# Four residual and four A12 buffers instead of two in the first down projection of a two-layer trunk

## Chip, cores and metric

The kernel runs on one core of one Trainium2 chip. The metric is the device time of one execution in microseconds (us); the median of three runs is given.

## What is computed

Two layers, each a mixer and a SwiGLU block, on 1024 tokens of width 1024 in float32. The reference, cut to what this change touches:

```python
def rmsnorm(x, g):
    y = x * lax.rsqrt(jnp.mean(x * x, axis=-1, keepdims=True) + RMS_EPS)
    return y * g
def swiglu(h, w_gate, w_up, w_down):
    return (jax.nn.silu(h @ w_gate) * (h @ w_up)) @ w_down
for layer in range(2):
    h = rmsnorm(x, norm_mix_pre[layer])
    m = attention_mixer(h, ...) if layer == 0 else recurrent_mixer(h, ...)
    x = x + rmsnorm(m, norm_mix_post[layer])
    h = rmsnorm(x, norm_ffn_pre[layer])
    x = x + rmsnorm(swiglu(h, ...), norm_ffn_post[layer])
```

The stage in question is the `@ w_down` of layer 0 with the norm and residual behind it, the pre-norm of layer 1's recurrent mixer, and that mixer's first projection (`h @ w_in`).

## The kernel before

Matrix products are done in float32 by splitting each operand into a high and a low half and adding three products (lines 748 to 750: high by high, high by low, low by high). The halves are made by a cast on ScalarE (ACT) and a subtraction on VectorE (DVE). A scheduler orders the instructions of each engine's queue from the program; buffers of a tag rotate, and an instruction that takes a buffer waits for the last reader of the tile that had it.

The down projection (`down`, lines 736 to 885) is one level of Strassen: seven products of 512 tokens by 512 columns with 11 steps of depth each. The first five (`p1`, `p6`, `p7`, `p5`, `p4`) leave the second half of the token rows (r = 1) finished, in four tiles `m2[0..3]` of 128 tokens. Each is then put through `norm(1, a, ...)`: `post_norm_of` (lines 234 to 263) loads the residual rows `x` (tag "nx", two buffers, line 241; line 196 issues the load), takes squares (ACT, line 178), gets 1/rms in two small instructions on GpSimd (POOL, lines 182 and 183), multiplies by the gain (DVE, line 250), adds the residual (DVE, line 256), stores `x` (line 258, SP's queue), and goes on to the pre-norm of the next mixer: squares of `x` (line 178), 1/rms, scaling (ACT, line 212), eight transposes on TensorE (PE, line 222, into two PSUM banks that rotate), a cast (ACT, line 57) and a subtraction (DVE, line 58) into `hT`.

While these norms run, PE does product `p3` (blocks S4, line 851, and w_down, line 855) and then the last product, token tile by token tile: for a = 0 to 3 the rows of A12 (from DRAM, line 875, tag "act", two buffers, three loads of 4, 4 and 3 blocks for each a) are split (ACT line 877, DVE line 878, into four buffers of tag "wb") and multiplied by the eleven split blocks `b21` (w_down, line 868), 33 matmuls for each a. DVE adds the result to `m1[a]` (line 883), and `norm(0, a, ...)` follows. Then the recurrent mixer starts: its weights are loaded (line 137, tag "raw", three buffers, shared with the loads of lines 851 and 868), scaled on DVE (line 151) or POOL (line 148), split (ACT line 155, DVE line 156), and the first projection (lines 166 to 168) multiplies them by `hT`: 72 matmuls on the first 512 tokens (a = 0 and 1), then 72 on the others (a = 2 and 3).

All loads and stores named here stand in SP's one queue, in the scheduler's order.

Of the kernel before, what the change touches and what calls it, by code (L numbers as in the profile page):

```python
# [8 lines left out]
F32 = mybir.dt.float32  # L9
# [6 lines left out]
P = 128  # L16
S = 1024
D = 1024
# [9 lines left out]
def rows(t, x):  # L28

    if not isinstance(t, tuple):  # L30
        return [(slice(0, P), x[t * P:(t + 1) * P, :])]
    r, a = t
    o = [2 * a * P + k * P + 64 * r for k in range(2)]
    return [(slice(64 * k, 64 * k + 64), x[o[k]:o[k] + 64, :]) for k in range(2)]


class HiddenT:


    def __init__(self, trunk, pool):  # L40
        self.nc = trunk.nc
        self.half = [tuple(pool.tile([P, KT, HALF], F32R, tag="hT", bufs=4, name=trunk.uid("hT"))
                           for _ in range(2)) for _ in range(2)]
# [56 lines left out]
class Trunk:  # L100
# [4 lines left out]
    def __init__(self, ctx, tc, io):  # L105
        self.ctx, self.tc, self.nc, self.io = ctx, tc, tc.nc, io
        nc = self.nc
        self.const = ctx.enter_context(tc.tile_pool(name="const", bufs=1))
        self.main = ctx.enter_context(tc.tile_pool(name="main", bufs=1))
        self.dram = ctx.enter_context(  # L110
            tc.tile_pool(name="dram", bufs=1, space=bass.MemoryType.DRAM))
        c = self.const
        self.ident = c.tile([P, P], F32, name="ident")
        make_identity(nc, self.ident)
        self.neghalf = c.tile([P, 1], F32, name="neghalf")
        nc.vector.memset(self.neghalf, -0.5)
        self.zero = c.tile([P, 1], F32, name="zero")
        nc.vector.memset(self.zero, 0.0)
        self.gcol = c.tile([P, 3, KT], F32, name="gcol")
        self.n = 0  # L120
        self.mark = None
        self.turned = {}
# [112 lines left out]
    def post_norm_of(self, ms, mg, x_src, x_dst, t, gpost, sink, pool, x=None):  # L235

        nc = self.nc
        if x is None:  # L240
            x = pool.tile([P, D], F32, tag="nx", bufs=2, name=self.uid("x"))
        for d, s in rows(t, x_src):
            self.load(x[d, :], s)
        junk = pool.tile([P, D // len(ms)], BF16, tag="junk", bufs=1, name=self.uid("junk"))

        squares_first = mg is ms[0][1] or len(ms) == 1
        if squares_first:
            rs = self.rstd(pool, [m for _, m in ms], junk)
        for c, m in ms:
            scaled = nc.vector.tensor_tensor(mg[:, c], m, gpost[:, c], op=ALU.mult).ins  # L250
        if not squares_first:
            rs = self.rstd(pool, [m for _, m in ms], junk)
        self.last_m = [self.squared, scaled]

        def rest(later=False):
            nc.vector.scalar_tensor_tensor(x, mg, rs, x, op0=ALU.mult, op1=ALU.add)
            for k, (d, s) in enumerate(rows(t, x_dst)):
                (nc.scalar if k and sink is None else nc.sync).dma_start(s, x[d, :])
            if sink is not None:
                return self.pre_norm(pool, x, mg, None, sink, t, self.psum_t, later)  # L260

        return rest
# [465 lines left out]
    def down(self, l, gO, x_src, x_dst, make_sink):  # L728
# [9 lines left out]
        def block(j, row, c0=0, n=D):  # L738
            return w[(2 * j + row) * P:(2 * j + row + 1) * P, c0:c0 + n]

        def split(pool, tag, bufs, src):
            t = pool.tile([P, 2, 512], F32R, tag=tag, bufs=bufs, name=self.uid("o"))
            nc.scalar.copy(t[:, 0], src)  # L743
            tt(t[:, 1], src, t[:, 0].bitcast(F32), op=ALU.subtract)  # L744
            return t

        def matmuls(ps, a, b, first, last):
            nc.tensor.matmul(ps, a[0], b[:, 0], start=first, stop=False)  # L748
            nc.tensor.matmul(ps, a[0], b[:, 1], start=False, stop=False)  # L749
            nc.tensor.matmul(ps, a[1], b[:, 0], start=False, stop=last)  # L750

        def product(operands, first=0):
            ps = [self.psum() for _ in range(4)]
            js = [*range(first, NP), *range(first)]
            for j in js:
                a, b = operands(j)
                for t in range(4):
                    tok = slice(t * P, (t + 1) * P)
                    matmuls(ps[t], (a[:, 0, tok], a[:, 1, tok]), b, j == js[0], j == js[-1])
            return ps  # L760

        main = self.main

        keep = make_sink is nullcontext
        with self.pool(f"d{l}") as ap, ExitStack() as right:
            m1, m2 = ([ap.tile([P, D], F32, tag="m", bufs=8, name=self.uid("m")) for _ in range(4)]
                      for _ in range(2))
# [68 lines left out]
            with make_sink() as sink:  # L836
                def norm(r, a, m):
                    ms, mg = [(slice(0, D), m)], m
                    if r == 0 and sink is None:
                        ms = [(c, m[:, c]) for c in (hi, lo)]  # L840
                        mg = ap.tile([P, D], F32, tag="mg", bufs=1, name=self.uid("mg"))

                    x = main.tile([P, D], F32, tag="raw", bufs=3, name=self.uid("x")) if keep and r == 0 else None
                    self.post_norm(ms, mg, x_src, x_dst, (r, a), gpost, sink, ap, x)

                for a in range(4):
                    norm(1, a, m2[a])

                def p3(j):
                    r = main.tile([P, 2, 512], F32, tag="raw", bufs=3, name=self.uid("raw"))  # L850
                    nc.sync.dma_start(r[:, 0], gO["S4"][j])
                    b22 = ts[j][:, 1]
                    if not keep:
                        b22 = r[:, 1]
                        nc.sync.dma_start(b22, block(j, 1, 512, 512))
                    return split(main, "w", 8, r[:, 0]), split(ap, "wb", 4, b22)

                for m, ps in zip(m1, product(p3)):
                    tt(m[:, hi], ps, m[:, hi], op=ALU.add)
                b21 = []  # L860
                for j in range(NP):
                    if keep:
                        src = ts[j][:, 0]
                    else:
                        if j % 2 == 0:
                            r = main.tile([P, 2, 512], F32, tag="raw", bufs=3, name=self.uid("raw"))
                        src = r[:, j % 2]
                        nc.sync.dma_start(src, block(j, 1, 0, 512))
                    b21.append(split(*((main, "w", 8) if j < 6 else (ap, "wc", 5)), src))
                for a in range(4):  # L870
                    ops = []
                    for j in range(0, NP, 4):
                        n = min(4, NP - j)
                        r = ap.tile([P, 4, P], F32, tag="act", bufs=2, name=self.uid("act"))[:, :n]
                        self.load(r, gO["A12"][:, j:j + n, a * P:(a + 1) * P])
                        t = ap.tile([P, 2, 4, P], F32R, tag="wb", bufs=4, name=self.uid("o"))
                        nc.scalar.copy(t[:, 0, :n], r)  # L877
                        tt(t[:, 1, :n], r, t[:, 0, :n].bitcast(F32), op=ALU.subtract)  # L878
                        ops += [(t[:, 0, i], t[:, 1, i]) for i in range(n)]
                    ps = self.psum()  # L880
                    for j in range(NP):
                        matmuls(ps, ops[j], b21[j], j == 0, j == NP - 1)
                    tt(m1[a][:, lo], ps, m1[a][:, lo], op=ALU.add)
                    norm(0, a, m1[a])
        self.mark = None


    def recurrent(self, ap, hT, yT):
# [275 lines left out]
```

## Time and profile before

| | us |
|---|---|
| median of 3 runs (lowest, highest) | 2204.94 (2204.70, 2206.01) |
| the profiled execution | 2205.06 |
| its span, first to last instruction | 2203.3 |
| TensorE busy in the span | 2170.1 |

Times inside the trace are us from the span's start. A matmul's record is longer than the step from one matmul to the next, since matmuls are pipelined; what PE takes is read from one start to the next. An ACT or DVE record likewise ends a little after the next one starts.

### The profile page before, as it was taken

To read this page: it belongs to the slowest core of one execution; us is meant where nothing else is said; L and a number is where in the kernel's file an instruction comes from. 1 tells how busy PE (TensorE), PEld (TensorE's weight loads), DVE (VectorE), ACT (ScalarE), POOL (GpSimd) and SP (SyncE) were. 2 spreads that over 40 slices of the span, in tenths; PEclk is the share of its full clock that TensorE was granted. 3 is DMA by queue.
4 is the path that set the end of the run, shared out by engine and by line. 5 is a ranking of instruction groups with operands and counts; after the bars stand their busy time and mean duration, and the time that the engine had idled before them with its cause. 6 is when DMAs were issued, how large, how long until landed. Compare 5 with 4: busy or idle time off the path is not lost.

```text
span 2203.3 us, 30597 instructions
## 1 busy us (share of the span) xinstructions
PE 2170.1 (98%) x11198; PEld 1811.7 (82%) x11198; DVE 1536.5 (70%) x2496; ACT 1143.0 (52%) x2108; POOL 228.2 (10%) x458
## 2 busy tenths in 40 slices
PE   8999999999999999999999999999999999999998
PEld 8898989878788888888887777887788888888886
DVE  6786765566868777676767677437777677768775
ACT  4545555466765444443446576527755444434543
POOL 3111112121100000000001332102100000000011
PEclk9999999999999999999999999999999999999999
DMA  5101011226323333336468421356233333328565
GB/s 177 54 30 35 25 54 38 65 85 219 137 91 101 117 95 119 96 129 229 144 181 251 127 62 40 95 195 222 81 111 106 95 120 96 120 95 287 170 179 158
DMA packets 184392, 266.03 MB, mean 121 GB/s; under 512 B 13617, under 2 KB 114993, under 8 KB 184242
## 3 DMA queue, kind: packets, MB, share of 16 engines
q1 hardware_dynamic: 183602, 261.98, 37.8%
q10 hardware_dynamic: 640, 2.10, 0.3%
q8 instruction: 88, 1.44, 0.3%
q14 instruction: 62, 0.51, 0.1%
HBM read 198.49 MB, written 65.54 MB: 120 GB/s over the span
## 4 chain that ended last, share of the span: by engine, by line
PE 85%; DVE 6%; ACT 3%; DMA 3%; issue 2%; POOL 1%; SPq 0%; POOLq 0%; ACTq 0%; DVEq 0%
PE ps L663 13%; PE ps L664 13%; PE ps L665 13%; PE ps L514 7%; PE ps L750 5%; PE ps L748 5%; PE ps L749 5%; PE psq L166 3%; PE psq L167 3%; PE psq L168 3%; PE pso L344 2%; PE tr L413 2%; PE ps L167 2%; PE ps L166 2%; PE ps L168 2%
## 5 line engine op out<-in xcount | busy, mean ns | idle before, releaser
L663 PE MATMUL ps<-hS,q 128*128 128x512 f32 (+1 forms) x1288 | 490.9, 382 | 0.3 <-ACT hS L96 0.3
L664 PE MATMUL ps<-hS,q 128*128 128x512 f32 (+1 forms) x1288 | 490.0, 381 | 0.9 <-DVE hS L89 0.9
L665 PE MATMUL ps<-hS,q 128*128 128x512 f32 (+1 forms) x1288 | 489.4, 380 | 0.0
L634 DVE TENSOR_TENSOR q<-raw,q 128x512 fp32r<-128x512 f32 x308 | 205.1, 688 | 191.8 <-ACT q L633 191.4
L664 PEld LDWEIGHTS ps<-hS,q 128*128 128x128 f32 x1288 | 243.3, 189 | 47.3 <-DVE hS L89 1.3
L663 PEld LDWEIGHTS ps<-hS,q 128*128 128x128 f32 x1288 | 243.0, 189 | 47.6 <-ACT hS L96 0.8
L665 PEld LDWEIGHTS ps<-hS,q 128*128 128x128 f32 x1288 | 243.2, 189 | 45.7
L633 ACT CAST q<-raw 128x512 fp32r<-128x512 f32 x308 | 177.0, 615 | 144.9 <-DVE raw L642 135.9
L749 PE MATMUL ps<-o,o 128*128 128x512 f32 x616 | 240.5, 391 | 0.2 <-DVE o L744 0.2
L750 PE MATMUL ps<-o,o 128*128 128x512 f32 x616 | 238.3, 390 | 0.0
L621 ACT ACTIVATE raw<-raw,gcol 128x256 f32<-128x256 f32 x352 | 150.2, 498 | 160.5 <-DMA raw<-in_ffn_w_up_dram 83.0
L748 PE MATMUL ps<-o,o 128*128 128x512 f32 x616 | 221.8, 392 | 3.0 <-ACT o L877 2.9
L743 ACT CAST o<-raw 128x512 fp32r<-128x512 f32 x184 | 110.4, 621 | 164.2 <-PE ps L750 48.8
L182 POOL TENSOR_SCALAR rs<-ss 128x1 f32<-128x1 f32 x60 | 35.3, 588 | 1445.8 <-ACT junk L178 1363.9
L744 DVE TENSOR_TENSOR o<-raw,o 128x512 fp32r<-128x512 f32 x184 | 123.6, 689 | 56.4 <-ACT o L743 55.5
L748 PEld LDWEIGHTS ps<-o,o 128*128 128x128 f32 x616 | 115.9, 188 | 29.1 <-ACT o L877 4.8
L156 DVE TENSOR_TENSOR wlo<-raw,whi 128x1024 fp32r<-128x1024 f32 x76 | 92.9, 1222 | 64.5 <-ACT whi L155 63.6
L749 PEld LDWEIGHTS ps<-o,o 128*128 128x128 f32 x616 | 116.1, 189 | 25.0 <-DVE o L744 1.1
L750 PEld LDWEIGHTS ps<-o,o 128*128 128x128 f32 x616 | 115.9, 188 | 24.3 <-DVE o L878 0.4
L155 ACT CAST whi<-raw 128x1024 fp32r<-128x1024 f32 x76 | 79.8, 1050 | 64.0 <-PE psq L167 23.6
L400 DVE TENSOR_TENSOR_SCAN pr<-pr,zero 128x128 f32<-128x128 f32 (+7 forms) x64 | 87.1, 1364 | 27.7 <-POOL pr L397 27.4
L166 PE MATMUL psq<-hT,whi 128*128 128x512 f32 x256 | 101.4, 396 | 1.1 <-DVE v L296 1.1
(202 smaller groups left out, 4298.8 us busy)
## 6 DMA issues: line engine op xcount, KB each, us to landing
raw<-in_ffn_w_gate_dram SPq DMA_DIRECT2D x44, 512.0 KB, 4.2
raw<-in_ffn_w_up_dram SPq DMA_DIRECT2D x44, 512.0 KB, 4.3
gS<-c SPq DMA_DIRECT2D x88, 256.0 KB, 3.8
raw<-gS SPq DMA_DIRECT2D x88, 256.0 KB, 2.8
gA<-c SPq DMA_DIRECT2D x66, 256.0 KB, 3.3
raw<-in_ffn_w_down_dram SPq DMA_DIRECT2D x63, 256.0 KB, 4.1
raw<-in_attn_w_in_dram SPq DMA_DIRECT2D x24, 512.0 KB, 3.9
raw<-gA SPq DMA_DIRECT2D x44, 256.0 KB, 2.8
```

Of the source, the lines that this page charges most:

```text
L166: nc.tensor.matmul(ps, wh[:, kt, cols], hh[:, kt, :], start=kt == 0, stop=False)
L514: self.matmul = nc.tensor.matmul(ps[:, n * 512:(n + 1) * 512], x, y[:, n, :], start=first and i == 0, stop=last and i == len(passes) - 1).ins
L621: nc.scalar.activation(raw[:, i], raw[:, i], AF.Copy, scale=gain[:, 4 * k + i:4 * k + i + 1])
L633: self.last = nc.scalar.copy(t[:, 0], src).ins
L634: self.last_lo = nc.vector.tensor_tensor(t[:, 1], src, t[:, 0].bitcast(F32), op=ALU.subtract).ins
L663: nc.tensor.matmul(ps, a[:, 0, kt, :], bh, start=kt == 0, stop=False)
L664: nc.tensor.matmul(ps, a[:, 0, kt, :], bl, start=False, stop=False)
L665: self.matmul = nc.tensor.matmul(ps, a[:, 1, kt, :], bh, start=False, stop=kt == 3).ins
L744: tt(t[:, 1], src, t[:, 0].bitcast(F32), op=ALU.subtract)
L748: nc.tensor.matmul(ps, a[0], b[:, 0], start=first, stop=False)
L749: nc.tensor.matmul(ps, a[0], b[:, 1], start=False, stop=False)
L750: nc.tensor.matmul(ps, a[1], b[:, 0], start=False, stop=last)
```

## The change

`self.nx` is the number of residual buffers, 2 everywhere but in the down projection of layer 0, where it is 4; there the A12 loads get 4 buffers as well. Nothing is computed otherwise. Lines 118 to 762 move down by one, those behind 764 by three.

```diff
@@ class Trunk, __init__
         nc.vector.memset(self.neghalf, -0.5)
+        self.nx = 2
@@ post_norm_of
-            x = pool.tile([P, D], F32, tag="nx", bufs=2, name=self.uid("x"))
+            x = pool.tile([P, D], F32, tag="nx", bufs=self.nx, name=self.uid("x"))
@@ down
         keep = make_sink is nullcontext
+
+        self.nx = 2 if keep else 4
...
-                        r = ap.tile([P, 4, P], F32, tag="act", bufs=2, name=self.uid("act"))[:, :n]
+                        r = ap.tile([P, 4, P], F32, tag="act", bufs=2 if keep else 4, name=self.uid("act"))[:, :n]
...
-        self.mark = None
+        self.mark, self.nx = None, 2
```

The scheduler orders several queues anew. Place 1 is DVE's queue in the last product, from the second weight tile of the recurrent mixer on (`raw_12072`; the third is `raw_12079`); `act_11884`, `act_11889` and `act_11892` are the A12 rows of a = 2, `m_10038` and `m_10039` are a = 0 and 1. Before:

```order
L151 TENSOR_TENSOR raw_12072<-raw_12072,gcol 128x1024
L156 TENSOR_TENSOR wlo_12069<-raw_12065,whi_12068 128x1024
L878 TENSOR_TENSOR o_11811<-act_11809,o_11811 128x384
L151 TENSOR_TENSOR raw_12079<-raw_12079,gcol 128x1024
L883 TENSOR_TENSOR m_10038<-ps_11731,m_10038 128x512
L878 TENSOR_TENSOR o_11884<-act_11882,o_11884 128x512
L250 TENSOR_TENSOR m_10038<-m_10038,g_10564 128x1024
L878 TENSOR_TENSOR o_11889<-act_11887,o_11889 128x512
L883 TENSOR_TENSOR m_10039<-ps_11814,m_10039 128x512
L256 SCALAR_TENSOR_TENSOR x_11766<-m_10038,rs_11770,x_11766 128x1024
```

And now:

```order
L152 TENSOR_TENSOR raw_12072<-raw_12072,gcol 128x1024
L157 TENSOR_TENSOR wlo_12069<-raw_12065,whi_12068 128x1024
L152 TENSOR_TENSOR raw_12079<-raw_12079,gcol 128x1024
L881 TENSOR_TENSOR o_11884<-act_11882,o_11884 128x512
L886 TENSOR_TENSOR m_10038<-ps_11731,m_10038 128x512
L881 TENSOR_TENSOR o_11889<-act_11887,o_11889 128x512
L881 TENSOR_TENSOR o_11894<-act_11892,o_11894 128x384
L886 TENSOR_TENSOR m_10039<-ps_11814,m_10039 128x512
L251 TENSOR_TENSOR m_10038<-m_10038,g_10564 128x1024
L881 TENSOR_TENSOR o_11967<-act_11965,o_11967 128x512
L257 SCALAR_TENSOR_TENSOR x_11766<-m_10038,rs_11770,x_11766 128x1024
```

The splits of a = 2 stand ahead of the norm of a = 0, but still behind the scaling of the third weight tile.

Place 2 is DVE's queue just before and at the first matmuls of the recurrent mixer; `pst_11785` and `pst_11790` are the transposes of a = 0, `pst_11868` and `pst_11873` those of a = 1 in the same two banks, and `m_10041` is a = 3. Before:

```order
L256 SCALAR_TENSOR_TENSOR x_11932<-m_10040,rs_11936,x_11932 128x1024
L156 TENSOR_TENSOR wlo_12083<-raw_12079,whi_12082 128x1024
L58 TENSOR_TENSOR hT_11292<-pst_11868,hT_11291 128x4x2x64
L156 TENSOR_TENSOR wlo_12305<-raw_12302,whi_12304 128x1024
L883 TENSOR_TENSOR m_10041<-ps_11980,m_10041 128x512
L58 TENSOR_TENSOR hT_11292<-pst_11873,hT_11291 128x4x2x64
```

And now:

```order
L157 TENSOR_TENSOR wlo_12305<-raw_12302,whi_12304 128x1024
L257 SCALAR_TENSOR_TENSOR x_11932<-m_10040,rs_11936,x_11932 128x1024
L58 TENSOR_TENSOR hT_11292<-pst_11785,hT_11291 128x4x2x64
L886 TENSOR_TENSOR m_10041<-ps_11980,m_10041 128x512
L58 TENSOR_TENSOR hT_11292<-pst_11790,hT_11291 128x4x2x64
L251 TENSOR_TENSOR m_10041<-m_10041,g_10564 128x1024
L58 TENSOR_TENSOR hT_11292<-pst_11868,hT_11291 128x4x2x64
L58 TENSOR_TENSOR hT_11292<-pst_11873,hT_11291 128x4x2x64
```

The subtraction that frees the banks of a = 0 has moved behind the weight splits and the residual of a = 2. On PE the transposes of a = 1, which stood eleven matmuls ahead of the mixer's first matmul, now stand directly ahead of it.

Place 3 is POOL's queue there; `raw_12378` and `raw_12480` are the fourth and the next weight tile of that mixer, `rs_11945` is the pre-norm of a = 2, `rs_12019` and `rs_12028` are the two norms of a = 3. Before:

```order
L148 TENSOR_SCALAR raw_12378<-raw_12378,gcol 128x128 x8
L182 TENSOR_SCALAR rs_11945<-ss_11946 128x1
L183 TENSOR_TENSOR rs_11945<-rs_11945,neghalf 128x1
L148 TENSOR_SCALAR raw_12480<-raw_12480,gcol 128x128 x8
L182 TENSOR_SCALAR rs_12019<-ss_12020 128x1
L183 TENSOR_TENSOR rs_12019<-rs_12019,neghalf 128x1
```

And now:

```order
L149 TENSOR_SCALAR raw_12378<-raw_12378,gcol 128x128 x8
L149 TENSOR_SCALAR raw_12480<-raw_12480,gcol 128x128 x8
L183 TENSOR_SCALAR rs_11945<-ss_11946 128x1
L183 TENSOR_SCALAR rs_12019<-ss_12020 128x1
L184 TENSOR_TENSOR rs_11945<-rs_11945,neghalf 128x1
L184 TENSOR_TENSOR rs_12019<-rs_12019,neghalf 128x1
```

The pre-norm of a = 2 now stands behind both weight tiles.

In SP's queue the residual loads of a = 2 and 3 (r = 1), 1 MB, have moved ahead of the first S4 block of `p3`, and the third and fourth A12 load, 0.45 MB, ahead of its fourth; the later residual and A12 loads have each moved up by two tiles, into the places that these left.

## Rows read from the trace of the kernel before

**Rows 1.** The page, part 1: busy us (share) and instructions of each engine.
```profile
PE 2170.1 (98%) x11198; PEld 1811.7 (82%) x11198; DVE 1536.5 (70%) x2496; ACT 1143.0 (52%) x2108; POOL 228.2 (10%) x458
```
**Rows 2.** Window: stretch, length, busy PE PEld DVE ACT POOL, clock, DMA share, GB/s.
```profile
1200.00:1225.00 25.00, 22.19 (x89) 16.61 (x89) 19.08 (x26) 11.98 (x22) 3.50 (x5) 0.93 0.79 192
```
**Rows 3.** Waits of PE's weight loads, 1196 to 1256: us in total, times, longest.
```profile
PEld ps L748 <- ACT o L877: 4.8, 5, 2.2
```
**Rows 4.** Timeline of PE: start us, us, what [idle before <- releaser].
```profile
1201.24 0.63 PE L222 MATMUL pst<-ident,m 128*128 128x128 f32 x4 [0.16 <-DVE hT L58]
1203.82 0.79 PE L748 MATMUL ps<-o,o 128*128 128x512 f32 x1 [1.95 <-ACT o L877]
...
1206.97 0.45 PE L748 MATMUL ps<-o,o 128*128 128x512 f32 x1
...
1208.41 0.39 PE L749 MATMUL ps<-o,o 128*128 128x512 f32 x1
1208.64 0.39 PE L750 MATMUL ps<-o,o 128*128 128x512 f32 x1
...
1216.61 0.62 PE L750 MATMUL ps<-o,o 128*128 128x512 f32 x2
...
1235.70 0.84 PE L166 MATMUL ps<-hT,whi 128*128 128x512 f32 x3
...
1254.58 0.85 PE L166 MATMUL ps<-hT,whi 128*128 128x512 f32 x3
```
**Rows 5.** One window early in p3, columns as in rows 2.
```profile
1150.00:1155.00 5.00, 5.00 (x24) 4.14 (x23) 1.40 (x3) 1.91 (x4) 0.00 (x0) 1.00 1.03 320
```
**Rows 6.** Timelines of ACT and DVE where p3's first operands come and p4 ends.
```profile
1152.95 3.23 ACT L743 CAST o<-raw 128x512 fp32r<-128x512 f32 x5 [4.05 <-DMA raw<-gS]
...
1161.30 0.68 DVE L833 TENSOR_TENSOR m<-m,ps 128x512 f32<-128x512 f32 x1
```
**Rows 7.** Timeline of DVE in the last product.
```profile
1213.55 1.22 DVE L151 TENSOR_TENSOR raw<-raw,gcol 128x1024 f32<-128x1024 f32 x1
1214.68 0.69 DVE L883 TENSOR_TENSOR m<-ps,m 128x512 f32<-128x512 f32 x1
1215.28 0.69 DVE L878 TENSOR_TENSOR o<-act,o 128x512 fp32r<-128x512 f32 x1
...
1231.77 1.22 DVE L250 TENSOR_TENSOR m<-m,g 128x1024 f32<-128x1024 f32 x1
1232.91 0.55 DVE L878 TENSOR_TENSOR o<-act,o 128x384 fp32r<-128x384 f32 x1
1233.45 1.29 DVE L256 SCALAR_TENSOR_TENSOR x<-m,rs,x 128x1024 f32<-128x1024 f32 x1
1234.65 1.22 DVE L156 TENSOR_TENSOR wlo<-raw,whi 128x1024 fp32r<-128x1024 f32 x1
```
**Rows 8.** Timeline of ACT in the last product.
```profile
1222.89 1.04 ACT L178 ACTIVATE junk<-m 128x1024 bf16<-128x1024 f32 x1
...
1223.93 0.60 ACT L877 CAST o<-act 128x512 fp32r<-128x512 f32 x1
1224.44 1.15 ACT L212 ACTIVATE m<-x,rs 128x1024 f32<-128x1024 f32 x1
```
**Rows 9.** Timeline of POOL.
```profile
1224.11 1.25 POOL L182 TENSOR_SCALAR rs<-ss 128x1 f32<-128x1 f32 x1 [0.17 <-ACT junk L178]
1225.45 0.86 POOL L183 TENSOR_TENSOR rs<-rs,neghalf 128x1 f32<-128x1 f32 x1
...
1236.05 3.88 POOL L148 TENSOR_SCALAR raw<-raw,gcol 128x128 f32<-128x128 f32 x8 [2.63 <-DMA raw<-in_rg_w_in_dram]
...
1243.18 3.86 POOL L148 TENSOR_SCALAR raw<-raw,gcol 128x128 f32<-128x128 f32 x8 [2.29 <-DMA raw<-in_rg_w_in_dram]
```
**Rows 10.** Timeline of SP's queue: issues of recurrent weight loads.
```profile
1231.88 0.38 SPq L137 DMA_DIRECT2D raw<-in_rg_w_in_dram x1
...
1235.97 0.79 SPq L137 DMA_DIRECT2D raw<-in_rg_w_in_dram x1
```

## The prediction

> **What bounds the kernel now.** The page's first part comes first: TensorE is busy 2170.1 of 2203.3 us [rows 1], so 33 us in which PE does nothing are all that any edit of buffers can win, and only PE's gaps count. Next, the windows of the down projection of layer 0 (1143 to 1255): up to 1196 PE's matmuls follow each other without a gap, so p3 hides everything there. The first slice with a loss is 1200 to 1225: PE is busy 22.19 of 25 us and the granted clock is 0.93 [rows 2]. Then who ends these gaps: between 1196 and 1256 the weight loads of the last product (L748) wait five times, 4.8 us in all, for the split of A12 rows on ACT (L877) [rows 3], and that split waits for its DMA. PE's timeline shows the worst: after transposes at 1201.24 nothing until 1203.82 [rows 4]. From there the clock falls to its lower level: the seven matmuls up to 1206.97 take 3.15 us, where the usual step of 0.23 (1208.41 to 1208.64 [rows 4]) would make 1.6. So 4.8 + 1.55 = 6.35 us are lost to late A12 rows. That is the ceiling of this edit, 0.29% of the span.
>
> **The change part by part.** No instruction is added or removed; two kinds of loads move up in SP's queue, and the scheduler's new order moves steps on DVE, ACT, POOL and PE.
>
> *A12 loads.* With four buffers the loads of the second token tile are issued some 40 us earlier, and from then on each is two loads ahead. I price all five waits at nothing: gain 6.35. The lower end is the same waits with another cause, that is 0.
>
> *Residual loads.* No wait in this stretch ends on such a load, so they win nothing directly. Their cost is that 1 MB of them and 0.45 MB of A12 now stand ahead of p3's blocks, where DMA is full already (share 1.03, 320 GB/s [rows 5]): 1.45 MB at 320 GB/s is 4.5 us. What hides it: p3's first blocks are there at 1152.95, while the product ahead of it ends around 1161.30 [rows 6], about 8 us later. Behind that, as many bytes move up in the full stretch as move out of it. I take 0; the bounds are a delay of 1.5 and a gain of 1.5 for the last w_down blocks, from one or two 256 KB loads more or less ahead of them at 320 GB/s (0.8 each). If the cover were gone, the 4.5 us would be PE's.
>
> *What is late next.* This is where I expect the gain to go. All of DVE's last part hangs on the third weight tile of the recurrent mixer: its buffer is that of the last w_down block, so its load cannot come before that block is split, and four A12 buffers do not change that. I walk the new order (places 1 and 2 of the change) from its scaling on, which I leave at 1213.55, as it was [rows 7]. Steps, from one start to the next [rows 7, 8]: DVE 0.6 for 512 columns, 0.54 for 384, 1.14 for 1,024, 1.2 for the residual; ACT 1.04 for squares, 0.51 for a split, 1.15 for scaling and about 1.05 for a weight cast; the POOL pair for 1/rms 2.2 while DVE is busy (1224.11 to 1226.31 [rows 9]).
>
> 1. DVE: scaling to 1214.7, then the low half of a = 2's first A12 rows to 1215.3. PE wants it after 46 matmuls (10.4 us) and some transposes (0.6 to 1.2) from 1201.24, at about 1212.6. So PE waits 2.7 us at a place where it did not wait, and does the matmul at 1215.3, against 1216.84 before (the second of the row at 1216.61 [rows 4]). Of 6.35, 1.5 is left.
> 2. DVE then takes in the result of a = 0 (1215.9), two splits and the result of a = 1 (1217.6), the gain (1218.7), a split, the residual of a = 0 (1220.5). ACT: squares of x and of a = 1 (1222.6), a split, scaling of a = 0 (1224.3), two weight casts (1226.4). DVE: gain and residual of a = 1 with a split and the result of a = 2 between (1226.1), two weight splits (1228.4). ACT: squares twice, a weight cast, and only then the cast of a = 0's first bank (1230.1) and scaling of a = 1 (1231.2). DVE: gain of a = 2, a weight split, residual of a = 2 (1232.0), and only then the subtraction that frees a = 0's first bank (1232.6) and, behind the result of a = 3, the second (1233.8).
> 3. PE ends a = 3 at 1215.3 + 64 x 0.227 + eight transposes (1.2) = 1231.0. The transposes of a = 1 now stand there with no matmul between them and the mixer; they wait for the two banks until 1232.6 and 1233.8. ACT, behind two more squares, casts at 1234.8: the mixer's first matmul comes then, against 1235.70 [rows 4]. Gain left: 0.9.
> 4. PE has then been idle for over 3 us around 1231 to 1234. Rows 4 show 1.55 us of slow clock after an idle time of 1.95, so the clock may fall here, for 1.55. The low half of `hT` comes behind one more gain on DVE, 0.4 later than before. POOL: the fourth weight tile can be issued at 1227.2 and lands 4.2 later, as from 1231.88 to 1236.05 [rows 9, 10]; the next, issued at 1228.4, lands by 1235.6 at its slowest, 7.2 as from 1235.97 to 1243.18; two blocks of 3.9 us end at 1239.5; the pair 1241.7, scaling of a = 2 1242.9. PE gets to its transposes at 1236.0 + 21 x 0.227 + 1.55 = 1242.3 and waits 0.6. What was waited for a = 3 before (0.5 at 1252.7) goes, since its norm no longer has the second weight tile to itself ahead of it.
>
> **Sum** at the first matmul on the second 512 tokens, 1254.58 before [rows 4]: -0.9 + 0.4 + 1.55 + 0.6 - 0.5 = +1.15. Without the slow clock it is the same, since PE then waits longer for the same scaling (2.1 instead of 0.6). If POOL's part is quicker than walked and the clock stays up, neither counts, and it is -0.9 + 0.4 - 0.5 = -1.0. Behind that point nothing of the change is left but some reordered matmuls of the same count. I take the middle, which is no change: the profiled execution's 2205.06 (0.12 over the median) stays, rounded to 2205.0. With 1.5 us for the blocks' landing and 1 us for the walk's rounding beyond -1.0 and +1.15, the forecast's own range is 2201.5 to 2208.7.
>
> **The rivals.**
>
> *The buffers pay in full.* DVE and ACT run ahead instead of behind, because the third weight tile lands earlier or its scaling costs PE nothing. PE then goes through 110 matmuls and 24 transposes from 1201.24 without a wait and reaches the mixer by 1229. Price: the whole 6.35, 2198.7. For it: the five waits are this operand's alone [rows 3]. Against it: DVE was busy 19.08 of 25 us in the very slice [rows 2], and its queue keeps the weight tile ahead of the A12 rows. The Trainium skill, page "Perfetto Trace Analysis", section Optimization Strategy, says that gaps that repeat on the engine that should be saturated can mean that there is too little memory for the next tile, buffer count being one cause; by that rule the added buffers would close the gaps, and this rival's time would hold. The trace agrees with it as to the cause of the five waits, not as to what comes behind them.
>
> *POOL makes it slower.* The pre-norm of a = 2 now stands on POOL behind both weight tiles (place 3). If the second of them is issued only when it was before, at 1235.97, since the weight splits that free its buffer slip, it lands at 1243.18 [rows 9, 10]; its block ends at 1247.1, the pair by 1249.3 and scaling 1.15 later, and PE stands at the transposes from about 1242.3 to some 1249.5 to 1250.5. Price: some 7 us, 2212. It decides from a landing after about 1235, for PE reaches the transposes at 1242.3 and the block, the pair and scaling take 3.9 + 2.2 + 1.15. For it: this load took 7.2 us. Against it: both weight splits on DVE now come right behind the residual of a = 1, 7 us earlier in the walk.
>
> That the change does not do what it says is ruled out by the order of SP's queue, where the loads have moved.
>
> **How the numbers follow.** About 0.2%, 4.4 us, is what a measurement of this kernel can tell from no change. Forecast 0.70, full gain 0.17, POOL 0.13. The forecast's range lies within 4.4 us of the median, so these are also the chances of no change, faster and slower. The range reaches down to the full gain, 2198.7, and up to the forecast's own end, 2208.7; the POOL case is left out.
>
> **What would show it.** Right, if the changed trace has no wait of L748's operands for A12 around 1203 and the clock stays up there; if a wait for an A12 split on DVE appears at a = 2's start near 1213; if the mixer's first matmuls come at 1234 to 1236 behind a gap of some 3 us at the transposes of a = 1, ended by ACT or DVE; and if the matmuls on the second 512 tokens start within 3 us of 1254.58. Wrong, if the mixer starts by 1231, if PE stalls for p3's blocks around 1161, or if over 4 us of PE's idle time end on POOL.

## The result, and the profile after

The changed kernel takes 2211.49 us (median of 7 runs, 2209.31 to 2213.21), the kernel before 2204.70 (7 runs beside them, 2202.54 to 2206.01). The ratio is 1.0034, with a 95% interval of 1.0025 to 1.0044: slower by about 7 us, where no change was forecast and the range ended at 2208.7. The profiled execution is the fastest of the seven, 2209.31.

The page's first part, columns as in rows 1:

```profile
PE 2170.8 (98%) x11198; PEld 1811.2 (82%) x11198; DVE 1536.8 (70%) x2496; ACT 1143.4 (52%) x2108; POOL 225.5 (10%) x458
```

The work is that of [rows 1] to within 0.7 us, but for POOL's, which is 2.7 less; what came is idle time of PE. To find where, I follow the start of the same matmul record through both traces. The 6,300th, some 73 us ahead of p3's first, starts at 1088.67 in the kernel before and at 1090.19 here. These 1.52 us arose in stages that the change does not touch (a second profile of the kernel before has 1.61), and I call such a difference a profile's shift. The 7,020th, in the mixer, starts at 1254.11 before and at 1261.23 here. Between the two PE takes 165.44 us before and 171.04 after: **+5.6 us, all of the change's loss that the trace shows.**

Windows of the changed kernel, columns as in rows 2:

```profile
1150.00:1155.00 5.00, 5.00 (x23) 4.13 (x22) 1.63 (x3) 0.53 (x1) 0.00 (x0) 1.00 1.02 230
1155.00:1160.00 5.00, 5.00 (x23) 4.13 (x22) 0.00 (x0) 0.52 (x1) 0.00 (x0) 1.00 1.03 289
1160.00:1165.00 5.00, 5.00 (x24) 4.14 (x23) 4.79 (x8) 3.20 (x6) 0.00 (x0) 1.00 1.12 323
1200.00:1225.00 25.00, 21.91 (x87) 16.16 (x86) 20.43 (x31) 12.53 (x23) 1.52 (x2) 0.93 0.94 248
1225.00:1250.00 25.00, 21.61 (x99) 17.03 (x98) 17.21 (x19) 16.48 (x25) 15.11 (x29) 0.93 0.45 128
```

The last window of the kernel before, which the prediction did not look at as a whole:

```profile
1225.00:1250.00 25.00, 24.02 (x115) 19.07 (x114) 15.96 (x19) 13.99 (x22) 12.96 (x26) 1.00 0.59 168
```

The slice from 1200 to 1225 is as bad as it was [rows 2]. The new loss is in the next one: 21.61 of 25 us against 24.02, 99 matmuls against 115, and a granted clock of 0.93 against 1.00. DMA is full from 1150 to 1165, where before it was full to 1160 ([rows 5]; its share from 1160 to 1165 was 0.60), while ACT and DVE stand almost still until 1159. PE feels nothing of that there: it is busy 5.00 of 5.00. It does later, from 1186 on (below).

SP's queue (start, us, what) and ACT's timeline, changed kernel:

```profile
1145.15 5.00 SPq L197 DMA_DIRECT2D x<-xs  x8
1150.57 0.80 SPq L854 DMA_DIRECT2D raw<-gS  x1
```
```profile
1159.48 4.05 ACT L744 CAST o<-raw 128x512 fp32r<-128x512 f32 x6 [8.95 <-DMA raw<-gS]
```

Eight row loads now stand ahead of p3's first block, and its first cast starts at 1159.48 against 1152.95 [rows 6]: 6.53 later, 5.0 less the shift. DVE 60 us further on:

```profile
1219.69 1.23 DVE L152 TENSOR_TENSOR raw<-raw,gcol 128x1024 f32<-128x1024 f32 x1
1220.84 0.69 DVE L881 TENSOR_TENSOR o<-act,o 128x512 fp32r<-128x512 f32 x1
```

The scaling of the third weight tile, 1213.55 in [rows 7], is at 1219.69: 4.6 later less the shift. That tile's load, in SP's queue before and now, is issued 3.3 later less the shift:

```profile
1207.36 0.37 SPq L137 DMA_DIRECT2D raw<-in_rg_w_in_dram  x1
```
```profile
1212.18 0.52 SPq L138 DMA_DIRECT2D raw<-in_rg_w_in_dram  x1
```

The delay of p3's first blocks was carried on, not absorbed. PE, changed kernel:

```profile
1186.39 1.26 PE L223 MATMUL pst<-ident,m 128*128 128x128 f32 x8 [0.48 <-DVE hT L58]
...
1195.51 0.66 PE L223 MATMUL pst<-ident,m 128*128 128x128 f32 x4 [1.18 <-DVE hT L58]
...
1207.08 0.65 PE L749 MATMUL ps<-o,o 128*128 128x512 f32 x1 [1.10 <-ACT o L880]
...
1221.58 0.50 PE L751 MATMUL ps<-o,o 128*128 128x512 f32 x1 [1.25 <-DVE o L881]
...
1233.27 1.03 PE L223 MATMUL pst<-ident,m 128*128 128x128 f32 x8
...
1239.88 0.63 PE L223 MATMUL pst<-ident,m 128*128 128x128 f32 x4 [2.60 <-DVE hT L58]
1241.07 0.80 PE L223 MATMUL pst<-ident,m 128*128 128x128 f32 x4 [0.57 <-DVE hT L58]
1242.10 1.65 PE L167 MATMUL ps<-hT,whi 128*128 128x512 f32 x3 [0.23 <-ACT hT L57]
```

The transposes of r = 1 already wait for banks in p3 (0.48 and 1.18), and PE comes to the last product's first matmul 3.1 us later than before, less the shift; in the second profile of the kernel before it is 1.9. In the last product one wait for an A12 split is left (1.10), one has come at a = 2's start (1.25), and the transposes of a = 1 wait 2.60 and 0.57 us for the banks of a = 0. The mixer's first matmul is at 1242.10 against 1235.70 [rows 4], 4.9 later less the shift.

The banks are free when DVE has subtracted. DVE, kernel before, then the changed one:

```profile
1228.75 0.68 DVE L58 TENSOR_TENSOR hT<-pst,hT 128x512 fp32r<-128x512 f32 x1
1229.68 0.69 DVE L58 TENSOR_TENSOR hT<-pst,hT 128x512 fp32r<-128x512 f32 x1 [0.25 <-ACT hT L57]
```
```profile
1237.85 1.28 DVE L257 SCALAR_TENSOR_TENSOR x<-m,rs,x 128x1024 f32<-128x1024 f32 x1 [0.77 <-POOL rs L184]
1239.05 0.68 DVE L58 TENSOR_TENSOR hT<-pst,hT 128x512 fp32r<-128x512 f32 x1
...
1240.25 0.68 DVE L58 TENSOR_TENSOR hT<-pst,hT 128x512 fp32r<-128x512 f32 x1
```

a = 0's subtractions now stand behind the residual addition of a = 2, which itself waits 0.77 us for POOL. ACT's order, which casts ahead of them, has moved too. Kernel before, then the changed one; `hT<-pst` is an eviction of a bank, `whi<-raw` a weight cast, L178 and L179 are squares:

```profile
1227.54 0.58 ACT L57 CAST hT<-pst 128x512 fp32r<-128x512 f32 x1
...
1229.07 0.58 ACT L57 CAST hT<-pst 128x512 fp32r<-128x512 f32 x1
...
1231.95 1.15 ACT L212 ACTIVATE m<-x,rs 128x1024 f32<-128x1024 f32 x1
...
1233.93 0.58 ACT L57 CAST hT<-pst 128x512 fp32r<-128x512 f32 x1
...
1235.36 0.59 ACT L57 CAST hT<-pst 128x512 fp32r<-128x512 f32 x1
1235.84 1.07 ACT L178 ACTIVATE m<-x 128x1024 f32<-128x1024 f32 x1
```
```profile
1235.53 0.58 ACT L57 CAST hT<-pst 128x512 fp32r<-128x512 f32 x1
1236.41 1.15 ACT L213 ACTIVATE m<-x,rs 128x1024 f32<-128x1024 f32 x1 [0.30 <-POOL rs L184]
1237.46 0.57 ACT L57 CAST hT<-pst 128x512 fp32r<-128x512 f32 x1
1239.17 1.06 ACT L179 ACTIVATE m<-x 128x1024 f32<-128x1024 f32 x1 [1.14 <-DVE x L257]
...
1240.42 1.06 ACT L179 ACTIVATE junk<-m 128x1024 bf16<-128x1024 f32 x1
...
1241.48 1.05 ACT L57 CAST hT<-pst 128x512 fp32r<-128x512 f32 x2
```

Before, a = 0's banks are evicted ahead of a = 1's scaling (1231.95), and a = 1's behind it with only weight casts between, at 1233.93 and 1235.36, ahead of a = 2's square. In the changed order a = 0's second eviction comes behind a = 1's scaling, and both of a = 1's (1241.48) behind two squares. The first of these waits 1.14 us for the residual addition of a = 2. That costs at most 1 us, an estimate: the first transposes of a = 1 end at 1240.51. On both engines the mixer, which needs a = 0 and a = 1 only, thus waits for a = 2. The Trainium skill, page "PSUM — Partial Sum Buffer", section Engine vs sequencer instructions, says that "ScalarE/VectorE/GpSimdE queues are strict FIFO"; the rows agree.

### The profile page after: what moved, and what is told of

It is laid out like the page before. It is cut to its first block, busy times and chain, and to the rows that moved or that the text cites. A ratio compares the mean times of both kernels' runs of the same rounds, so it can differ in the third digit from the quotient of the medians.

```text
span 2207.5 us, 30582 instructions
## 1 busy us (share of the span) xinstructions
PE 2170.8 (98%) x11198; PEld 1811.2 (82%) x11198; DVE 1536.8 (70%) x2496; ACT 1143.4 (52%) x2108; POOL 225.5 (10%) x458
## 4 chain that ended last, share of the span: by engine, by line
PE 86%; DVE 5%; DMA 3%; ACT 2%; issue 2%; POOL 1%; SPq 0%; POOLq 0%; ACTq 0%; DVEq 0%
PE ps L664 12%; PE ps L665 12%; PE ps L666 12%; PE ps L515 8%; PE ps L749 5%; PE ps L750 5%; PE ps L751 5%; PE psq L167 3%; PE psq L168 3%; PE psq L169 3%; PE ps L167 2%; PE ps L168 2%; PE ps L169 2%; PE pso L345 2%; PE tr L414 2%
```

## The experiments

All runs in one table. "Stage" is PE's time from its 6,300th to its 7,020th matmul record in that run's profile, against 165.44 us in the first profile of the kernel before. The ratio is against runs of the kernel before on the same chip; x4, a4, x4late and after_again ran on one chip, x4fix and beforefix on another, the others on a third.

| run | x rows / A12 buffers, and what else | ratio (95%) | stage |
|---|---|---|---|
| after_again | 4 / 4, the change | 1.0035 (1.0022 to 1.0048) | +5.5 |
| x4 | 4 / 2 | 1.0019 (1.0011 to 1.0028) | +4.5 |
| a4 | 2 / 4 | 1.0021 (1.0012 to 1.0031) | +4.3 |
| x4late | 4 / 4, rows behind three S4 blocks | 1.0027 (1.0017 to 1.0037) | +5.7 |
| dose | 2 / 2, two tiles' rows loaded twice | 1.0021 (1.0012 to 1.0029) | +2.1 |
| late | 4 / 4, weights ahead of rows and A12 | 1.0030 (1.0018 to 1.0041) | +5.2 |
| afterdve | 4 / 4, weight scalings later | 1.0034 (1.0021 to 1.0046) | +5.2 |
| a4dve | 2 / 4, weight scalings later | 1.0017 (1.0008 to 1.0026) | +4.6 |
| before_again | 2 / 2, the kernel before | 0.9999 (0.9990 to 1.0007) | +0.2 |
| afterturn | 4 / 4, evictions in the old place | 1.0008 (0.9999 to 1.0016) | +2.3 |
| afterfix | 4 / 4, evictions and weights | 1.0003 (0.9994 to 1.0012) | -1.6 |
| a4fix | 2 / 4, evictions and weights | 0.9987 (0.9978 to 0.9996) | -2.8 |
| x4fix | 4 / 2, evictions and weights | 1.0017 (1.0006 to 1.0027) | +3.6 |
| beforefix | 2 / 2, evictions and weights | 1.0016 (1.0006 to 1.0026) | +1.7 |

The stage's end lies inside the mixer, and the last four runs move two transposes behind it. At the 7,200th record, 40 us on, afterfix stands at -0.9, a4fix at -2.1, x4fix at +4.3, beforefix at +2.4 and afterturn at +2.7; the others are within 0.2 of the table.

**The two halves apart (x4, a4).**

```diff
-r = ap.tile([P, 4, P], F32, tag="act", bufs=2 if keep else 4, ...)
+r = ap.tile([P, 4, P], F32, tag="act", bufs=2, ...)
```
and for a4 instead
```diff
-self.nx = 2 if keep else 4
+self.nx = 2
```

> The change's first half alone: four buffers for the residual rows, two for A12. Theory A (the residual rows of a=2 and 3, 1 MB, are now loaded ahead of the S4 blocks of the next product, and that product's casts, the normalizations, the stores and the weight loads behind them all come about 5 us later): the first S4 cast starts 4 to 6.5 us later than in the kernel before, and the time is 3 to 8 us over the kernel before, as the whole change's 6.8 us. Theory B (the loss is in what the scheduler did with the A12 splits, the weight tile and the banks; the early loads are hidden): within 1.5 us of the kernel before.

> The change's second half alone: two buffers for the residual rows, four for A12. Theory A: the first S4 cast starts where it does in the kernel before (within 1.5 us), the three waits for A12 splits (4.8 us) go, a wait at a=2's start and one ahead of the mixer come, and the time is between 4 us under the kernel before and 1 us over it. Theory B: 4 to 8 us over the kernel before, as the whole change.

Neither theory had both halves lose, and both do, by about 4 us. In x4 the first S4 cast comes 4.7 us late less the shift, in a4 only 0.5, so each has its own way to lose. What they share is the third weight tile's scaling on DVE, 1.8 late in x4 and 2.1 in a4 less the shifts, and waits ahead of the mixer. These two sizes are only some 1 us above what one kernel's own profiles differ by (before_again, below).

**Which bytes? (x4late, dose).** The rows of a = 2 and 3 behind the first three S4 blocks; and, in the kernel before, 1 MB more:

```diff
+if not keep and a == 2:
+    early = [s4(j) for j in range(3)]
+    self.mark = early[2][1]
 norm(1, a, m2[a])
```
```diff
-for d, s in rows(t, x_src):
+for d, s in rows(t, x_src) + (rows(t, x_src) if sink is not None and t in ((1, 0), (1, 1)) else []):
     self.load(x[d, :], s)
```

> The whole change, but the residual rows of a=2 and 3 are loaded behind the first three S4 blocks instead of ahead of them; the same bytes. Theory A in its narrow form (what counts is that the first S4 blocks wait): the first S4 cast comes 3 us or more earlier than in the changed kernel and the time falls by 3 to 6 us, to within 3 us of the kernel before. Theory A in its wide form (the DMA engines are full there, and any bytes put into that stretch push all blocks behind them): the first cast is earlier, the later ones are not, and the time stays within 1.5 us of the changed kernel. Theory B: no change against the changed kernel.

> The kernel before, with two buffers of each as it was, but the residual rows of r=1, a=0 and 1 are loaded twice: 1 MB more through the DMA engines at the stage's start, nothing else. Theory C (in the runs so far the mixer's first matmul comes 20.7 to 21.6 us after the DVE addition of a=0, L883 in the kernel before, and that addition stands on DVE behind the scaling of the third mixer weight tile, which lands later by the bytes that are put ahead of it): at the 290 to 350 GB/s of that stretch 1 MB takes 3.0 to 3.6 us, so the third tile's scaling, the addition and the mixer come 2 to 4 us later, and the time is 2 to 4.5 us over the kernel before. Theory D (the loss is made by the new order of A12 splits and banks, and the loads have slack): within 1 us of the kernel before.

x4late's first cast is back at 1158.12 (its shift is 4.67, so +0.5), and its time is not: the narrow form has fallen, what counts is not the first blocks. dose, whose order around the mixer's start is that of the kernel before but for a pair of neighbours on ACT and on DVE, puts a price on late loads. Its SP queue and DVE:

```profile
1145.92 9.01 SPq L196 DMA_DIRECT2D x<-xs  x8
```
```profile
1219.83 1.23 DVE L151 TENSOR_TENSOR raw<-raw,gcol 128x1024 f32<-128x1024 f32 x1 [0.55 <-DMA raw<-in_rg_w_in_dram]
```

Less its shift of 2.28 the scaling is 4.0 late, the mixer's first matmul (1240.54) 2.6, and the stage 2.1 us longer; the time's interval is 2.6 to 6.4 us. **A hold-up of the loads at that place is paid for in the mixer's start**, as expected. It is no price of the bytes alone: the second load of a tile waits until the first has landed, some 4.8 us of the 9.01 in SP's queue, where the changed kernel's eight loads take 5.00. p3's first block is issued 6.5 late less the shift, against 2.9 there, and the order in p3 differs too. So far theory C, in which the late tile sets everything, looked right.

**The control (after_again).**

> The changed kernel itself, on the same chip as the others: 5 to 8.5 us over the kernel before, and where the profiled execution's matmuls fall behind the kernel before tells whether the 2.9 us that the first profile won back around 1550 us belong to the change or to the execution.

The stage repeats within 0.2 us. The 2.9 us that the first profile won back around 1550 are not the change's (below).

**Freeing the chain of the late tile (late, afterdve, a4dve).** `late` loads the three mixer tiles ahead of the rows of r = 0, a = 2 and 3 and of the later A12 rows; the other two move two DVE scalings behind the residual addition of a = 1:

```diff
+self.w_raw = [self.raw(io["rg_w_in"][:, 1024 + c * P:1024 + (c + 1) * P]..., KT) for c in range(3)]
...
+self.mark = near if keep or (a, j) <= (1, 0) else self.raw_dma[1]
 self.load(r, gO["A12"][:, j:j + n, a * P:(a + 1) * P])
...
+self.mark = near if keep or a < 2 else self.raw_dma[2]
 norm(0, a, m1[a])
```
```diff
-ws = {c: w_load(1024 + c * P, len(cs) == 1) for c in cs}
+for c in cs:
+    with self.tc.issue_after(self.second) if c in (1, 2) else nullcontext():
+        ws[c] = w_load(1024 + c * P, len(cs) == 1)
```

> The whole change, but the three mixer weight tiles' loads stand ahead of the residual rows of r=0, a=2 and 3 (1 MB) and of the A12 loads behind the fourth; those loads now follow the second or third tile. Theory C: the third tile's scaling and a=0's addition come 2.5 us or more earlier than in the changed kernel, against the stage's start, the mixer's first matmul stays 21 us behind the addition, and the time falls by 2.5 to 6 us against the changed kernel. Theory D: the order of the splits at the mixer is still the changed one, so the time stays within 1.5 us of the changed kernel.

> The whole change, all loads in its order, but on DVE the scalings of the second and third mixer weight tiles stand behind the residual addition of a=1 instead of ahead of a=0's addition. Theory C: a=0's addition no longer waits for the third tile and comes 3 to 6 us earlier, the waits ahead of the mixer's first matmul (5 to 6 us) shrink to under 3, and the time falls by 3 to 8 us against the changed kernel, to between 2 us under and 2 us over the kernel before. Theory D: within 2 us of the changed kernel, since splits and banks are the changed ones. A third way: the second or third tile is then late for the mixer's second or third group, and what is won at the first is lost at the next.

> Four buffers for A12, two for the residual rows, and the same move of the two scalings on DVE. Theory C: against the kernel before 2 to 6 us faster: the waits for A12 splits are gone (4.8 us and slow clock 1.5), the addition of a=0 comes no later than in the kernel before, and the mixer no later than PE can finish. Theory D: 2 us or more over the kernel before, as with the A12 buffers alone.

All three miss the time that theory C expected. In `late` the tile's scaling is back (1214.41, shift 0.43), but PE now waits 2.98 us for the A12 rows that were held back, so it is no clean test. a4dve has no such wait. Its DVE, ACT and PE (shift 2.47):

```profile
1229.88 2.36 DVE L151 TENSOR_TENSOR raw<-raw,gcol 128x1024 f32<-128x1024 f32 x2
```
```profile
1230.00 1.06 ACT L178 ACTIVATE m<-x 128x1024 f32<-128x1024 f32 x1 [1.67 <-DVE x L256]
...
1233.17 1.16 ACT L212 ACTIVATE m<-x,rs 128x1024 f32<-128x1024 f32 x1 [0.93 <-POOL rs L183]
1234.23 1.03 ACT L155 CAST whi<-raw 128x1024 fp32r<-128x1024 f32 x1
1235.16 0.57 ACT L57 CAST hT<-pst 128x512 fp32r<-128x512 f32 x1
```
```profile
1237.26 0.63 PE L222 MATMUL pst<-ident,m 128*128 128x128 f32 x4 [2.04 <-DVE hT L58]
1238.99 1.04 PE L222 MATMUL pst<-ident,m 128*128 128x128 f32 x4 [1.10 <-DVE hT L58]
```

The scaling of a = 1, at 1230.70 less the shift, is 1.25 us *earlier* than the 1231.95 before, so the chain up to there is cured. But a = 0's first eviction follows it, where it had stood 4.4 us ahead of it, and the transposes of a = 1 wait 2.04 and 1.10 for the banks. No wait of PE's ends on a weight tile, so the moved scalings did not come too late for the mixer. But they now take 2.36 us of DVE ahead of the subtractions that free the banks, so this run alone doesn't say that the order of the evictions costs whatever the tile does. Theory C, in which the tile is all, fell; theory E puts the order first, and the next runs test it.

**The evictions in their old place (before_again, afterturn, afterfix, a4fix).** afterturn is the whole change with edges within engines only:

```diff
-self.post_norm(ms, mg, x_src, x_dst, (r, a), gpost, sink, ap, x)
+rest = self.post_norm_of(ms, mg, x_src, x_dst, (r, a), gpost, sink, ap, x)
+behind = []
+if sink and r == 0 and a:
+    behind = sink.done[0, 0][:1] if a == 1 else sink.done[0, 1]
+with self.behind(behind):
+    rest()
...
+with self.behind([self.turned[0, 0]] if sink and a == 3 and j else ()):
     matmuls(ps, ops[j], b21[j], j == 0, j == NP - 1)
```

(`sink.done[r, a]` holds the last eviction of that tile on ACT and on DVE.) afterfix and a4fix add, for the second and third weight tile:

```diff
+with self.behind([self.second] if c in (1, 2) else ()):
+    ws[c] = w_load(1024 + c * P, len(cs) == 1, hT.done[0, 1] if c in (1, 2) else ())
```
where the last argument holds the casts and splits behind a = 1's evictions (the first gate tile's too).

> The kernel before itself: another profiled execution, within 0.1% of its own runs. It tells how far the stage's PE waits, the place of a=0's addition and the 2.9 us around 1550 us vary between executions of one kernel. Both theories: the stage's waits within 1 us of the first profile's; if they differ by more, the profiles' differences of 2 to 5 us tell less than they seem to.

> The whole change, its loads and DVE scalings where it has them, but the evictions of the turned residual rows (ScalarE casts and VectorE splits into hT) of a=0 and a=1 stand about where the kernel before has them: a=0's ahead of the square of a=1's new residual, a=1's ahead of a=2's residual addition and squares, and a=0's transposes ahead of a=3's second group of matmuls. Theory E (with more A12 splits done early the schedule puts a=1's evictions behind a=2's squares, one of which waits for a=2's residual addition, so the mixer's first matmul waits for a=2 where before it waited for a=1): the waits ahead of the mixer fall from 5 to 6 us to under 3 and the time falls 2 to 4 us against the changed kernel. Theory F (it is the bytes alone: everything behind the late third weight tile is late, whatever the order): within 1 us of the changed kernel.

> As the run before, and also the scalings of the second and third mixer weight tiles behind a=1's residual addition and their casts behind a=1's evictions, so that nothing of the chain to the mixer stands behind a late tile. Theories E and F together (half order, half bytes by way of the tile): a=0's addition 3 us or more earlier than in the changed kernel, a=1's evictions straight behind their transposes, waits ahead of the mixer under 2 us, time between 3 us under and 1.5 us over the kernel before. E alone: as the run with the evictions only. F alone: no better than the changed kernel by more than 2 us, as the move of the scalings alone was.

> Four buffers for A12 and two for the residual rows, with the same order as the run before. If the order is what the A12 buffers cost (theory E), their own gain shows: 1 to 5 us under the kernel before, mixer's first matmul at the end of the A12 product with under 1.5 us of waits. Theory F: as the A12 buffers alone, 3 us or more over the kernel before.

The kernel before repeats its stage within 0.2 us; inside it the first cast comes 1.1 later than in the first profile, less the shift, and the third tile's scaling 0.8. afterturn, with the same loads and the same late tile as the changed kernel, has 1.0008 for 1.0034 and +2.3 for +5.6: more than half of the loss was the order. Its PE (shift 1.82) goes from the transposes of a = 1 to the mixer with 0.24 of a wait:

```profile
1239.11 1.04 PE L224 MATMUL pst<-ident,m 128*128 128x128 f32 x8
1240.38 0.97 PE L168 MATMUL ps<-hT,whi 128*128 128x512 f32 x3 [0.24 <-ACT hT L57]
```

afterfix takes the late tile off the path as well, and the stage is 1.6 us *shorter* than before. The move of the scalings was worth 0.4 us of the stage with the evictions in the wrong order; with them in the right one, and the casts behind them, it is worth 3.9 (3.6 at the 7,200th record). The two delays lay on parallel paths to one point: curing the tile alone only showed the other, while curing the order alone gave more than half. How much of the 3.9 is the casts' and how much the scalings' was not separated. a4fix, which leaves out the residual buffers and so 1 MB of early loads, beats the kernel before, ratio 0.9987 (0.9978 to 0.9996). Its PE and ACT (shift 0.54):

```profile
1232.09 1.03 PE L225 MATMUL pst<-ident,m 128*128 128x128 f32 x8
1233.36 0.51 PE L169 MATMUL ps<-hT,whi 128*128 128x512 f32 x1 [0.24 <-ACT hT L57]
```
```profile
1230.80 1.14 ACT L215 ACTIVATE m<-x,rs 128x1024 f32<-128x1024 f32 x1
1232.72 1.07 ACT L57 CAST hT<-pst 128x512 fp32r<-128x512 f32 x2 [0.79 <-PE pst L225]
1233.68 2.96 ACT L158 CAST whi<-raw 128x1024 fp32r<-128x1024 f32 x3
```

Scaling, transposes, evictions, mixer, with the three weight casts behind them: the mixer starts 2.9 us earlier than in [rows 4], less the shift.

**Whose gain is it? (x4fix, beforefix).** The order of afterfix with the other two pairs of buffers.

> The residual rows' four buffers alone, with the order of evictions, casts and scalings of the two runs before. Theory E with bytes: the order costs nothing any more, what is left is the price of 1 MB of rows ahead of the blocks and weights (between 1 and 4 us by the run that loaded rows twice), less what the order itself gives: within 0 to 3 us over the kernel before, and 2 to 5 us over the A12 buffers with the same order. If the residual buffers pay once the order is right: under the kernel before.

> The kernel before with that order, two buffers of each. If the 3.4 us that the A12 buffers won under the new order are the A12 buffers' own: within 1.5 us of the kernel before, with the waits for A12 splits (4 to 5 us at the A12 product's start) still there. If they are the order's: 2 us or more under the kernel before, like the A12 buffers with that order.

The order alone gains nothing: beforefix is slower than the kernel before by some 3.5 us, which neither expectation had. With two A12 buffers the A12 splits on DVE cannot run ahead and stand behind the moved scalings, and PE waits for one of them at a = 3:

```profile
1232.97 0.80 PE L755 MATMUL ps<-o,o 128*128 128x512 f32 x1 [2.35 <-DVE o L888]
```

x4fix has the same wait (2.30). So under this order four A12 buffers are worth 3 to 6 us (0.9987 against 1.0016; 1.0003 against 1.0017, whose intervals overlap). These pairs compare two chips, each by its own runs of the kernel before. The residual buffers gain nothing by the ratio with two A12 buffers (1.0017 against 1.0016) and cost some 3.5 us with four (1.0003 against 0.9987, intervals that just touch); by the stage they cost 1.9 and 1.2.

## Why the prediction was wrong

- **The sum's failing term is the residual and early A12 loads, "I take 0".** The cover was real: PE is busy 5.00 of 5.00 in every window from 1150 to 1165, with the casts 5 us late. But the cover was PE's alone, and lasted for PE only to 1186. ACT, DVE and SP had no such slack: each does what follows in its order, so the delay went on into the third weight tile, whose scaling the walk left "at 1213.55, as it was". It was 4.6 late. The bounds of 1.5 either way counted only "one or two 256 KB loads more or less" ahead of the last w_down blocks; ahead of the third weight tile there were two tiles of residual rows (1 MB) and three A12 loads (0.7 MB) more. dose shows 4.0 us of lateness behind 1 MB more and the waits that came with it. With the measured start the sum's +1.15 becomes +5.8; at its point, the first matmul on the second 512 tokens, the changed kernel is at 1261.68, 5.6 late less the shift.
- **The walk behind it was right in kind.** It put the mixer's first matmul 21.25 us behind the start of that scaling (1213.55 to 1234.8), with a gap at the transposes of a = 1 ended by the banks and a slow clock behind it; measured are 22.4 (1219.69 to 1242.10) and waits of 2.60 and 0.57 for `hT` on DVE, then a granted clock of 0.66 from 1240 to 1245. So of the +4.9 at the mixer against its -0.9, the start gave 4.6 and the walk's own error 1.2. That the order there eats the gain, which the walk said, afterturn confirms.
- **A12 loads, gain 6.35: not in full.** The size was too big from the start: [rows 3] count waits of the weight loads, while PE's own idle time before these matmuls is 2.9 us in the kernel before (window 1196 to 1236):

```profile
PE ps L748 <- ACT o L877: 2.9, 3, 2.0
```

In the changed kernel one of the five waits is left (1.10 of PE's idle time, 1.5 as rows 3 count), and the clock still falls behind it: the granted clock of the slice is 0.93 again, as in [rows 2]. The 2.7 us predicted at a = 2's start were 1.25, since PE itself came later.

- **POOL** ended no wait of PE's, as forecast. Indirectly it has 0.77 us in the wait for a = 0's banks, by the residual addition of a = 2. "POOL makes it slower" had a time near the measured one, 2212, by luck: its reason, PE held by the pre-norm of a = 2, is not in the trace.
- **"The buffers pay in full"** asked that the tile land earlier or its scaling cost nothing. The Trainium skill's rule that stood beside it (page "Perfetto Trace Analysis", section Optimization Strategy: repeated gaps can mean too few buffers) did not hold for the change, 1.0034, nor for the A12 buffers alone, 1.0021; with the order repaired the same buffers give 0.9987.

What stays open: the ratios' differences, in us, lie between 0.9 below and 2.5 above the stage's (dose: +2.1 in the stage, 4.6 by the ratio). One profile for each run and scatter outside the stage don't tell more. How much of the residual buffers' price is bytes and how much is order was not separated: dose adds waits to the bytes, and the other runs with these buffers change the order as well.

## What to carry to other kernels

A buffer that lets a load start early also puts its bytes ahead of others: in a stretch where DMA is full, follow the delay through the queue of every engine behind it, not only to the engine that has slack. In a kernel whose order a scheduler sets, read the new order on the evicting engines at the next hand-over; a step that waits for a later tile, put ahead of an eviction, can cost more than the buffers give. Where two late things meet at one point, curing one can show little (0.4 us for the tile here): test both together before either is called harmless.

## What was not expected

Two profiles of one kernel differ by over 3 us at one place. From its 8,100th to its 8,400th matmul record (from about 1503 us on, in a later stage) PE took 67.6 us in the first profile of the kernel before and 64.1 in the second; in the changed kernel 64.7 in the first and 67.4 in the second. In the runs it goes by the chip and not by the kernel: all eight profiles from one chip (before_again, dose, late, afterdve, a4dve, afterturn, afterfix, a4fix) have 64.1 to 64.8, all six from the two others 67.1 to 67.6. The first two profiles' chip is not on record, and why the chips differ stays open. A single pair of profiles would have put 3 us there on the change, and it has no part in them; the stage itself repeats within 0.2 us.
